# Eight tables that set the order of the engine calls in a four-layer diffusion step, replaced by others

## The chip, the cores and the metric

The kernel runs on one core of one Trainium2 chip. The metric is the device time of one execution in microseconds (us). Before the change it is 3068.2 us, the median of three runs (3067.97 to 3069.68). Five engines work side by side, each through its own queue of instructions, in the order in which they were put there: TensorE (PE in the rows) multiplies matrices, VectorE (DVE), ScalarE (ACT) and GpSimd (POOL) work elementwise, SyncE (SP) issues most of the transfers. An instruction that waits for another engine holds up all that stands behind it in its own queue.

## The reference

One inference step over 640 tokens of 1024 features (128 context tokens, 512 latent tokens) in fp32, four layers with the mixers A, B, C, A, and an MLP after each:

```python
for i in range(DEPTH):                       # 4 layers; kind = i % 3: A, B, C, A
    sh, sc, gt, sh2, sc2, gt2 = split(silu(cond) @ w_ada[i] + b_ada[i], 6)   # for c_ctx and for c
    h = rmsnorm(x, norm_g[i, 0]) * (1 + sc) + sh
    # A: sliding-window GQA with a sink logit; B: latent attention (low-rank q and kv);
    # C: GQA with q and k normalised per head; all with rotary positions, 16 heads
    x = x + gt * (mixer(h) @ w_o)
    h2 = rmsnorm(x, norm_g[i, 1]) * (1 + sc2) + sh2
    x = x + gt2 * (square(relu(h2 @ w_mlp_in[i])) @ w_mlp_out[i])
y = rmsnorm(x, g_final)
```

The outputs are y for both groups of tokens and the new keys, values and latents of the context tokens.

## The kernel before

x lies in SBUF with the features on the partitions, 4 tiles of 2 x 320 tokens per half. Each matrix product goes in 128x128 weight tiles against 320 tokens (a half of the 640), and each fp32 product is three matmuls of reduced-precision parts: high by high, high by low, low by high. `Stream` carries the weights: SP loads 128x1024 of them into one of two buffers `wraw`, ACT rounds them to the high part (`wa<-wraw`, called "hi" below), DVE subtracts to get the low part (`wa<-wraw,wa`, "lo"), and PE runs 24 matmuls for one output tile and half ("a unit", 8 feature tiles times 3). A `wraw` buffer is free for the next load when its lo is done. Results stand in eight PSUM tiles (`ps`, `psl`) until DVE or ACT has read them.

The adaLN rows need 512 KB tiles of `w_ada` (`adaw`). In layer 0's start PE multiplies them (16 tiles, then 24 tiles `adan` during the projections that follow). From layer 0's output projection on, DVE does this beside the rest: per tile two reductions `junk<-adaw,cb`, one for each condition; POOL issues those loads.

A layer is split into phases, named in the code: "start" and "qkv" (the norm and the projections; layer 0 also "qkv2", mixer B "dq"), "attn", "oproj" (output projection, the next norm, the first MLP products), and the rest of the MLP, which belongs to no phase. `Kern.ordered` keeps all engine calls of a phase as a list, where consecutive calls of PE into the same PSUM tile form one item, and `Calls.replay` issues them in the order of a table of item numbers:

```python
def replay(self, order):
    kept, self.kept = self.kept, None
    for i in order or range(len(kept)):
        for c in kept[i][1]:
            self.make(*c)
...
order = ORDER.get(n) or n[2:] == "attn" and range(len(self.nc.kept))
```

The table holds for PE, DVE, ACT and POOL, and in "0 start" and "0 qkv" for SP too. For "1 attn" there is no table before: its 1344 items go in the order in which the planner of the attention wrote them (`PLAN`, `PairB`). All calls pass through one line, `Calls.make`, so every row of the profile has the line L276, and instructions are told apart by the tiles they write and read. Waits between engines follow from the data: a reorder changes no arithmetic and no tile, only who stands ahead of whom.

Of the kernel before, what the change touches and what calls it, by code (L numbers as in the profile page):

```python
# [41 lines left out]
ORDER = {  # L42
    "0 attn": """
# [20 lines left out]
    "0 oproj": """  # L64
# [9 lines left out]
    """,  # L74
    "0 qkv2": """
# [4 lines left out]
    """,  # L80
    "0 qkv": """
# [5 lines left out]
    """,  # L87
    "0 start": """
# [4 lines left out]
    """,  # L93
    "1 dq": """
# [6 lines left out]
    """,  # L101
    "1 oproj": """
# [9 lines left out]
    """,  # L112
    "2 attn": """
# [90 lines left out]
}  # L204
ORDER = {n: [int(i) for i in o.split()] for n, o in ORDER.items()}

# [1554 lines left out]
```

## Time and profile before

| | |
|---|---|
| median of three runs | 3068.2 us |
| the profiled execution | 3069.06 us, of which the span of the page is 3067.3 us |
| mean granted clock of TensorE | 0.991 of full speed |
| PE, DVE, ACT, POOL busy | 97%, 69%, 44%, 18% of the span |

The share is over the whole span. The phases run one after another, and only in those where PE has holes can an order gain or lose. A row of the timeline reads: start, duration, engine, line, operation and tiles, count, and in brackets the idle time before it and what ended that.

### The profile page before, as it was taken

The numbers are of one execution on the slowest core, as the hardware profiler recorded it, in microseconds if no ns is written. First come the engines' busy times: TensorE is split into PE (matmuls) and PEld (weight loads), VectorE is DVE, ScalarE is ACT, GpSimd is POOL, SyncE is SP. The second block draws the span as 40 slices with busy tenths as digits, with TensorE's granted clock in tenths as the row PEclk, the third lists the DMA queues.
The fourth block names the chain that finished last, engine by engine and source line by source line (L and its number), as shares of the span: only waits on it lengthen the run. The fifth ranks groups of instructions, "written<-read, shape, count | busy, mean of one in ns | idle before, by whom it ended". The sixth has DMA issues, their size and how long they took to land. (4 is left out here: it accounts for less than half of the span.)

```text
span 3067.3 us, 52256 instructions
## 1 busy us (share of the span) xinstructions
PE 2962.0 (97%) x20250; PEld 2884.7 (94%) x20250; DVE 2122.7 (69%) x4605; ACT 1339.0 (44%) x2836; POOL 548.0 (18%) x713
## 2 busy tenths in 40 slices
PE   6999999999999999999998999999999999999998
PEld 4888999999999989999997889999999899999998
DVE  5696767666788887767469988776747896533434
ACT  3384522323487753322347883332233593322331
POOL 1162000000044341000003660000000370000000
PEclk9999999999999999999999999999999999999999
DMA  8303344442121134444211013444431102222221
GB/s 300 130 1 124 103 145 152 149 149 96 40 60 47 37 125 163 147 152 148 84 55 45 10 43 118 146 150 152 144 93 49 46 1 83 90 72 74 76 76 49
DMA packets 88602, 300.72 MB, mean 98 GB/s; under 512 B 10977, under 2 KB 15281, under 8 KB 87969
## 3 DMA queue, kind: packets, MB, share of 16 engines
q1 hardware_dynamic: 64112, 210.22, 20.6%
q0 software_dynamic: 24240, 87.16, 8.7%
q8 instruction: 159, 2.61, 0.3%
q14 instruction: 91, 0.74, 0.1%
HBM read 288.53 MB, written 3.56 MB: 95 GB/s over the span
## 5 line engine op out<-in xcount | busy, mean ns | idle before, releaser
L276 PE MATMUL ps<-ar,wa 128*128 128x320 f32 x6736 | 1139.2, 311 | 16.4 <-DVE wa L276 8.7
L276 PE MATMUL psl<-ar,wa 128*128 128x320 f32 x6408 | 1084.3, 310 | 1.9 <-DVE ar L276 1.6
L276 PEld LDWEIGHTS ps<-ar,wa 128*128 128x128 f32 x6736 | 1030.0, 189 | 20.9 <-DVE wa L276 9.5
L276 PEld LDWEIGHTS psl<-ar,wa 128*128 128x128 f32 x6408 | 979.4, 188 | 3.4 <-DVE ar L276 2.3
L276 ACT ACTIVATE wa<-wraw 128x1024 fp32r<-128x1024 f32 (+3 forms) x350 | 360.0, 1030 | 965.2 <-PE psl L276 440.2
L276 DVE TENSOR_TENSOR wa<-wraw,wa 128x1024 fp32r<-128x1024 f32 (+3 forms) x346 | 416.7, 1204 | 291.8 <-ACT wa L276 290.8
L276 DVE CUSTOM_DVE_ANT_0 junk<-adaw,cb 128x1024 bf16<-128x1024 f32 x304 | 373.4, 1228 | 9.4 <-DMA adaw<-ada 8.9
L276 PE MATMUL psl<-ex,wa 128*128 128x320 f32 x1320 | 322.9, 314 | 5.1 <-DVE wa L276 2.0
L276 PE MATMUL ps<-ex,wa 128*128 128x320 f32 x1304 | 318.1, 313 | 5.5 <-DVE wa L276 3.3
L276 POOL TENSOR_TENSOR p<-p,st 128x640 f32<-128x640 f32 (+2 forms) x256 | 277.0, 1104 | 180.0 <-DVE st L276 144.7
L276 POOL DMA_DIRECT2D adaw<-ada x152 | 80.5, 530 | 1051.4 <-DVE mod L276 983.9
L276 PE MATMUL psl<-wa,ar 128*128 128x320 f32 (+3 forms) x1024 | 236.2, 335 | 17.0 <-DVE st L276 7.5
L276 PEld LDWEIGHTS psl<-ex,wa 128*128 128x128 f32 x1320 | 229.1, 189 | 9.4 <-DVE wa L276 2.3
L276 DVE TENSOR_TENSOR ar<-ps,ar 128x512 fp32r<-128x512 f32 (+3 forms) x416 | 223.2, 560 | 19.8 <-ACT ar L276 16.3
L276 PEld LDWEIGHTS ps<-ex,wa 128*128 128x128 f32 x1304 | 225.5, 189 | 9.8 <-DVE wa L276 4.2
L276 ACT ACTIVATE ar<-ps 128x512 fp32r<-128x512 f32 (+5 forms) x452 | 208.5, 489 | 56.1 <-PE ps L276 50.7
L276 DVE SCALAR_TENSOR_TENSOR x<-ps,mod,x 128x320 f32<-128x320 f32 (+2 forms) x264 | 107.2, 436 | 180.8 <-PE ps L276 180.6
L276 DVE SCALAR_TENSOR_TENSOR x<-psl,mod,x 128x320 f32<-128x320 f32 (+2 forms) x240 | 98.7, 436 | 192.3 <-PE psl L276 192.2
L276 ACT ACTIVATE p<-p,st 128x640 f32<-128x640 f32 (+2 forms) x256 | 190.6, 748 | 18.7 <-DVE st L276 8.6
L276 PEld LDWEIGHTS psl<-wa,ar 128*128 128x128 f32 x1024 | 166.0, 193 | 30.7 <-DVE st L276 14.9
L276 PE MATMUL ps<-cst,p 128*128 128x128 f32 x1088 | 155.2, 274 | 5.6 <-DVE wa L276 2.6
L276 DVE TENSOR_TENSOR usq<-relu 128x320 f32<-128x320 f32 x256 | 124.5, 487 | 44.5 <-ACT relu L276 42.6
(205 smaller groups left out, 2817.6 us busy)
## 6 DMA issues: line engine op xcount, KB each, us to landing
adaw<-ada POOLq DMA_DIRECT2D x152, 512.0 KB, 4.3
wraw<-win SPq DMA_DIRECT2D x128, 512.0 KB, 3.3
wraw<-wout SPq DMA_DIRECT2D x128, 512.0 KB, 3.3
wraw<-qkv SPq DMA_DIRECT2D x36, 512.0 KB, 3.6
wa<-adan SPq DMA_DIRECT2D x24, 512.0 KB, 5.1
wraw<-wo SPq DMA_DIRECT2D x24, 512.0 KB, 3.7
adaw<-ada SPq DMA_DIRECT2D x16, 512.0 KB, 8.4
ar<-wa SPq DMA_DIRECT2D x64, 80.0 KB, 2.1
```

What stands on the lines that cost most here:

```text
L276: return m(*a, **k)
```

## The change

The code stays; the dictionary `ORDER` changes. Eight of its tables hold other numbers: "0 start", "0 qkv", "0 qkv2", "0 oproj", "1 oproj", "2 qkv", "3 qkv", and "1 attn", which had none. The tables of the other phases ("0 attn", "1 dq", "2 attn", "2 oproj", "3 attn", "3 oproj") only stand elsewhere in the dictionary. The same instructions are issued, each as often as before.

```diff
 ORDER = {
...
+    "1 attn": """
...
-    "0 oproj": """
...
+    "0 oproj": """
...
```

Three places as the engines' queues have them. First SP at the very start of the program: `adaw` are the eight buffers for tiles of `w_ada` (the last number tells the buffer, 152 to 159), `x` the input in four pieces, `wraw` the first projection weights. Before:

```order
1 L276 DMA cst<-cst 128x384
2 L276 DMA adaw_3_155<-ada 128x1024
3 L276 DMA x<-x 128x4x320
...
5 L276 DMA wraw_0_61<-qkv 128x1024
...
7 L276 DMA adaw_1_153<-ada 128x1024
8 L276 DMA adaw_2_154<-ada 128x1024
9 L276 DMA x<-x 128x4x320 x3
10 L276 DMA wraw_1_62<-qkv 128x1024
11 L276 DMA adaw_0_152<-ada 128x1024
12 L276 DMA adaw_5_157<-ada 128x1024
13 L276 DMA adaw_4_156<-ada 128x1024
```

After:

```order
1 L316 DMA cst<-cst 128x384
2 L316 DMA adaw_0_152<-ada 128x1024
...
4 L316 DMA adaw_1_153<-ada 128x1024
5 L316 DMA adaw_2_154<-ada 128x1024
6 L316 DMA adaw_3_155<-ada 128x1024
7 L316 DMA adaw_4_156<-ada 128x1024
8 L316 DMA x<-x 128x4x320 x2
9 L316 DMA adaw_5_157<-ada 128x1024
...
13 L316 DMA adaw_0_152<-ada 128x1024
14 L316 DMA wraw_0_61<-qkv 128x1024
15 L316 DMA adaw_1_153<-ada 128x1024
```

The tile that PE takes first, adaw_0, moved from behind all four pieces of x and two weights to the front; two pieces of x moved far behind.

Second, DVE at the head of layer 0's output projection ("0 oproj"). `wa_1006` and `wa_111` are the lows of two weight pieces, the rows with `adaw` the reductions. Before:

```order
517 L276 TENSOR_TENSOR ar_87<-ps_74,ar_86 128x512
518 L276 TENSOR_TENSOR ar_87<-ps_72,ar_86 64x128 x2
519 L276 ISA junk,mod_0_169<-adaw_0_2674,cb 128x1024
...
533 L276 ISA junk,mod_0_169<-adaw_3_2677,cb 128x1024
534 L276 ISA mod_0_169 128x1
535 L276 TENSOR_TENSOR wa_1006<-wraw_1_62,wa_1005 128x1024
536 L276 SCALAR_TENSOR_TENSOR x<-psl_2_80,mod_0_166,x 128x192
537 L276 TENSOR_TENSOR wa_111<-wraw_0_61,wa_110 128x1024
```

After:

```order
519 L316 TENSOR_TENSOR wa_111<-wraw_0_61,wa_110 128x1024
520 L316 TENSOR_TENSOR ar_87<-ps_74,ar_86 128x512
521 L316 TENSOR_TENSOR ar_87<-ps_72,ar_86 64x128 x2
522 L316 ISA junk,mod_0_169<-adaw_0_2674,cb 128x1024
...
536 L316 ISA junk,mod_0_169<-adaw_3_2677,cb 128x1024
537 L316 ISA mod_0_169 128x1
538 L316 SCALAR_TENSOR_TENSOR x<-psl_3_81,mod_0_166,x 128x320
539 L316 SCALAR_TENSOR_TENSOR x<-psl_2_80,mod_0_166,x 128x192
540 L316 SCALAR_TENSOR_TENSOR x<-psl_1_79,mod_0_166,x 128x320
541 L316 TENSOR_TENSOR wa_1006<-wraw_1_62,wa_1005 128x1024
```

The low wa_111 went ahead of the eight reductions, wa_1006 stayed behind them with three reads of PSUM now ahead of it. On PE the two units that use wa_111 now stand ahead of the unit that uses wa_1006.

Third, DVE at the end of layer 3's projections ("3 qkv"), around the last two lows, wa_1006 and wa_111; the other rows are rotary products and sums (`rps`, `rpq`, `ar`). Before:

```order
3707 L276 SCALAR_TENSOR_TENSOR ar_97<-rpq_0_21710,ar_97 64x320
3708 L276 TENSOR_TENSOR rpq_1_21711<-rpq_1_21711,rps_1_21709 128x192
3709 L276 STREAM_SHUFFLE rps_0_21708<-ps_71 128x320
3710 L276 TENSOR_TENSOR rpq_0_21710<-ps_71,tab_0_21700 128x320
3711 L276 SCALAR_TENSOR_TENSOR ar_97<-rpq_1_21711,ar_97 64x320
3712 L276 SCALAR_TENSOR_TENSOR ar_96<-rpq_1_21711,ar_96 64x320
3713 L276 TENSOR_TENSOR rpq_0_21710<-rpq_0_21710,rps_0_21708 128x320
3714 L276 STREAM_SHUFFLE rps_1_21709<-ps_72 128x192
3715 L276 TENSOR_TENSOR rpq_1_21711<-ps_72,tab_0_21700 128x192
3716 L276 TENSOR_TENSOR wa_111<-wraw_1_62,wa_110 128x1024
```

After:

```order
3710 L316 TENSOR_TENSOR wa_1006<-wraw_0_61,wa_1005 128x1024
3711 L316 TENSOR_TENSOR wa_115<-ck_1_21705,wa_1004 128x128
3712 L316 TENSOR_TENSOR rpq_0_21710<-rpq_0_21710,rps_0_21708 128x320
3713 L316 TENSOR_TENSOR wa_117<-ck_0_21704,wa_113 128x128
3714 L316 STREAM_SHUFFLE rps_0_21708<-ps_71 128x320
3715 L316 TENSOR_TENSOR wa_111<-wraw_1_62,wa_110 128x1024
3716 L316 TENSOR_TENSOR rpq_1_21711<-rpq_1_21711,rps_1_21709 128x192
3717 L316 TENSOR_TENSOR wa_116<-ck_0_21704,wa_112 128x128
3718 L316 STREAM_SHUFFLE rps_1_21709<-ps_72 128x192
```

Between the two lows stood thirteen rotary instructions; now four short ones stand there. On ACT the hi of wa_111 (`wa_110`) went ahead of the roundings of `ar_96` and `ar_97` in the same way.

## Rows read from the trace of the kernel before

**Rows 1.** The page's first part: busy time, share, instructions.

```profile
PE 2962.0 (97%) x20250; PEld 2884.7 (94%) x20250; DVE 2122.7 (69%) x4605; ACT 1339.0 (44%) x2836; POOL 548.0 (18%) x713
```

**Rows 2.** Stretches: before PE, start, qkv, qkv2, 0 oproj, MLP, 1 attn, 1 oproj, 2 qkv, 3 qkv.

```profile
core 0: us, PE busy (x) PEld busy (x) DVE busy (x) ACT busy (x) POOL busy (x), PEclk, DMA share, GB/s
0.00:20.49 20.49, 0.00 (x0) 0.03 (x1) 3.78 (x13) 6.58 (x13) 1.97 (x7) 1.00 0.93 329
20.49:55.60 35.11, 30.70 (x252) 22.08 (x253) 24.93 (x66) 14.37 (x33) 4.80 (x9) 0.95 0.85 310
55.60:104.46 48.86, 43.52 (x416) 34.08 (x415) 31.47 (x76) 18.64 (x42) 7.34 (x9) 1.00 0.73 253
104.46:153.80 49.34, 45.60 (x291) 45.07 (x290) 37.87 (x92) 21.37 (x51) 11.97 (x15) 0.93 0.18 60
252.85:386.75 133.90, 126.13 (x845) 124.80 (x844) 96.31 (x198) 52.27 (x105) 6.36 (x12) 0.96 0.40 135
386.75:782.60 395.85, 395.85 (x2701) 395.43 (x2700) 266.44 (x486) 109.99 (x176) 25.87 (x49) 1.00 0.40 132
841.12:1090.85 249.73, 238.58 (x1761) 233.36 (x1761) 211.92 (x512) 194.96 (x458) 113.26 (x105) 1.00 0.17 46
1090.85:1187.75 96.90, 93.23 (x625) 91.02 (x626) 85.88 (x169) 48.03 (x96) 30.33 (x29) 1.00 0.48 166
1580.23:1699.30 119.07, 103.38 (x654) 94.65 (x653) 106.84 (x243) 79.24 (x186) 38.45 (x44) 0.99 0.15 48
2342.55:2441.81 99.26, 91.35 (x618) 89.35 (x617) 81.04 (x207) 45.75 (x108) 20.96 (x30) 0.95 0.19 57
```

**Rows 3.** PE's waits from 0 to 56 us: for whom, total, times, longest.

```profile
PE ps L276 <- DMA adaw<-ada: 23.6, 2, 20.5
```

**Rows 4.** DMA from 2 to 40 us: GB/s in 40 slices, then the sum.

```profile
GB/s 317 372 255 238 293 361 385 408 404 391 365 365 364 365 375 403 414 405 405 405 414 293 341 310 259 276 323 375 410 414 423 423 418 410 397 405 410 410 414 410
DMA packets 5609, 14.08 MB, mean 371 GB/s; under 512 B 653, under 2 KB 2849, under 8 KB 5608
```

**Rows 5.** PE's waits in "0 qkv" (55.6 to 104.5 us).

```profile
PE ps L276 <- DMA wa<-adan: 2.4, 3, 1.1
```

**Rows 6.** PE's timeline at the end of "0 qkv2".

```profile
137.97 1.93 PE L276 MATMUL ps<-ar,wa 128*128 128x320 f32 x12
...
144.21 0.90 PE L276 MATMUL ps<-ex,wa 128*128 128x320 f32 x2 [3.34 <-DVE wa L276]
...
147.04 3.40 PE L276 MATMUL ps<-ar,wa 128*128 128x320 f32 x12
```

**Rows 7.** DVE's timeline at the same place: the low.

```profile
142.94 1.22 DVE L276 TENSOR_TENSOR wa<-wraw,wa 128x1024 fp32r<-128x1024 f32 x1
```

**Rows 8.** PE's timeline in "0 oproj", 262 to 292 us.

```profile
270.46 3.98 PE L276 MATMUL ps<-ar,wa 128*128 128x320 f32 x26
281.09 11.20 PE L276 MATMUL ps<-ar,wa 128*128 128x320 f32 x57 [6.66 <-DVE wa L276]
```

**Rows 9.** DVE's timeline there, first reduction and low; a group of the page's part 5.

```profile
269.80 1.23 DVE L276 CUSTOM_DVE_ANT_0 junk<-adaw,cb 128x1024 bf16<-128x1024 f32 x1 [5.18 <-DMA adaw<-ada]
...
279.82 1.22 DVE L276 TENSOR_TENSOR wa<-wraw,wa 128x1024 fp32r<-128x1024 f32 x1
...
L276 DVE SCALAR_TENSOR_TENSOR x<-psl,mod,x 128x320 f32<-128x320 f32 (+2 forms) x240 | 98.7, 436 | 192.3 <-PE psl L276 192.2
```

**Rows 10.** DVE's waits in "1 attn": for whom, total, times, longest.

```profile
DVE wa L276 <- ACT wa L276: 12.8, 17, 2.0
DVE ar L276 <- ACT ar L276: 6.9, 16, 1.1
```

**Rows 11.** The late part of "2 qkv" as a stretch, columns as in Rows 2.

```profile
1650.00:1699.30 49.30, 40.66 (x269) 37.27 (x268) 45.74 (x99) 32.92 (x75) 17.43 (x20) 0.98 0.16 56
```

**Rows 12.** PE's waits in "3 qkv" (2342 to 2442 us).

```profile
PE psl L276 <- ACT wa L276: 3.3, 1, 3.3
PE psl L276 <- DVE wa L276: 2.8, 2, 1.5
```

More of the change, by code (lines that the diff above doesn't have):

```diff
@@ L42 @@
 ORDER = {
+    "2 attn": """
[21 rows of a table added]
+    """,
+    "1 attn": """
[38 rows of a table added]
+    """,
+    "1 oproj": """
[9 rows of a table added]
+    """,
+    "1 dq": """
[6 rows of a table added]
+    """,
+    "3 qkv": """
[9 rows of a table added]
+    """,
+    "2 qkv": """
[13 rows of a table added]
+    """,
+    "0 oproj": """
[9 rows of a table added]
+    """,
+    "0 qkv2": """
[4 rows of a table added]
+    """,
+    "0 qkv": """
[5 rows of a table added]
+    """,
+    "0 start": """
[4 rows of a table added]
+    """,
     "0 attn": """
@@ L63 @@
     """,
-    "0 oproj": """
[9 rows of a table removed]
-    """,
-    "0 qkv2": """
[4 rows of a table removed]
-    """,
-    "0 qkv": """
[5 rows of a table removed]
-    """,
-    "0 start": """
[4 rows of a table removed]
-    """,
-    "1 dq": """
[6 rows of a table removed]
-    """,
-    "1 oproj": """
[9 rows of a table removed]
-    """,
-    "2 attn": """
[21 rows of a table removed]
-    """,
     "2 oproj": """
@@ L145 @@
         323 300 339 335 301 337 322 336 324 314 316 325 315 346 330 317 331 338 340 341 332 333
-    """,
-    "2 qkv": """
[13 rows of a table removed]
     """,
@@ L191 @@
         277 289 288 282 299 300 294 283 284 285 290 301 305 295 297 302 317 306 312 303 313 315 314 296 298 316 307 308 309 318 319 310 311
-    """,
-    "3 qkv": """
[9 rows of a table removed]
     """,
```

198 rows, old and new, of the table ORDER are left out of this document.

## The prediction

> **What bounds the kernel now.** I read the page's busy shares first: PE works 97% of the span, the next engine 69% [rows 1]. So the time is PE's work plus PE's holes, and since the change adds and removes no instruction, it can only act on holes and on the clock that follows them. Then I cut the span into the phases whose tables change and took, in each, the length less PE's busy time [rows 2]: 20.49 us before the first matmul, then 4.41 in the start, 5.34 in "0 qkv", 3.74 in "0 qkv2", 7.77 in "0 oproj", 11.15 in "1 attn", 3.67 in "1 oproj", 15.69 in "2 qkv" (with the wait at its end, by which "2 attn" starts), 7.91 in "3 qkv". The MLP's stretch has none. Behind the first matmul that makes 59.7 us. The clock column adds to it: where it says 0.93, 0.96 and 0.95, TensorE ran part of the stretch at 1.2 instead of 2.4 GHz, (1 - 0.93) / 0.5 x 49.34 = 6.9 us of "0 qkv2", by the same sum 10.7 us of "0 oproj" and 9.9 us of "3 qkv". Last I read, in each phase, for whom PE waited; these rows are named with the terms. The sum below is made against the profiled execution, 3069.06 us; the median is 0.86 lower.
>
> **The change, phase by phase.** Negative is time saved.
>
> *Start.* PE's first matmul waits 20.5 us for a tile `adaw`, and again 3.1 later [rows 3]. Nothing is idle there but PE: the transfers run all the while, 14.08 MB from 2 to 40 us at 371 GB/s on the mean, and 397 to 423 GB/s in the last slices [rows 4]. The changed SP order puts adaw_0 to adaw_4 first and half of x behind the second group. PE then works on each tile as it lands and gives the buffers back early, so the dip in the middle of the GB/s row (259 to 341), which I read as SP waiting for a free buffer, should close. At 410 GB/s the same 14.08 MB take 34.3 us instead of 38: the last tile lands 3.7 us earlier, and PE's products of the normed x, which no longer queue behind the tiles' matmuls, close up some 1.3 us of the 4.41 of holes. I take -5. Bounds: 0 (transfers no denser, the same bytes) and -8 (3.7 + 4.41).
> The Trainium skill ("DMA: Bandwidth & Descriptors", "Where 436 GB/s comes from") says that transfers from HBM to SBUF are bound by about 358 GB/s per core, below the ceiling of the on-chip fabric. By that the stretch, already at 371, would gain nothing and the sum would be 5 less. The rows with 397 to 423 GB/s speak against it, so it gets no case of its own.
>
> *"0 qkv".* 2.4 of the 5.34 are waits for tiles `adan` [rows 5], which the new table spreads out earlier. Four buffers go round, so a tile's load still waits for PE's use of the one before. I take -3, between -5.3 and +1.
>
> *"0 qkv2".* PE waits 3.34 for a low that DVE starts at 142.94 [rows 6, 7]. In the new order five short DVE instructions that stood ahead of that low stand behind it, and about two others now come ahead of it; at 0.44 us for a pass over 320 columns [rows 9] that is 3 x 0.44 = 1.3 us, and the wait of the first of them for ACT falls away. I put the low 1.9 us earlier. At half clock the 12 matmuls at 147.04 took 3.40 instead of 1.93 at full clock, and the 12 before them 147.04 - 144.21 = 2.83, so the dip cost about 2.4. Whether a hole of 1.5 to 2 still brings it, the rows don't decide. I take -2.5: the hole's part and a quarter of the dip. Bounds 0 and -6.1 (3.7 + 2.4).
>
> *"0 oproj".* The one large hole. DVE does eight reductions from 269.80 on, 10.0 us with what follows, and only then the low that PE waits for: 6.66 us [rows 8, 9]. PE had stopped at 274.44, with two units left over that need only wa_111, whose hi and load are long there. The change puts wa_111's low ahead of the reductions, where DVE sat idle 5.18 us, and it puts these two units ahead on PE: 48 matmuls x 0.153 us (3.98 / 26 [rows 8]) = 7.3 us more work, up to 281.8. Behind the reductions three reads of PSUM of 0.44 us and the low of 1.22 end at 279.82 + 1.3 + 1.22 = 282.3; with some 0.3 us from DVE to PE that leaves about 1 us of wait, so -5.6. The dip behind the hole goes too: 57 matmuls in 11.20 us against 57 x 0.153 = 8.7, so -2.5. Also, wa_111's buffer `wraw` is free 16 us earlier, so the next weights come earlier. -8.1, of which I take -7.5 for other small waits. Bounds -2 (the hole reappears at the next low) and -10.2 (6.66 + 1.1 for the phase's other holes + 2.5).
>
> *"1 attn".* 11.15 us of holes in many places; DVE waits 17 times for ACT's rounding (12.8 us) and 16 times for ACT's rows `ar` (6.9) [rows 10]. In 249.73 us PE works 238.58, DVE 211.92 and ACT 194.96 [rows 2]: these three hand each other short pieces, and a table replaces the planner's order. The moves are mostly of a few places; a unit of the values goes ahead of the score units in several spots, which fills holes of about 1 us. No row shows the new order's waits. Bounds -11 (all holes) and +8 (12.8 + 6.9 again by four tenths); I take -3, near the middle of the bounds.
>
> *"1 oproj".* A one-row sum behind an elementwise add went behind a unit on PE, and the order of the norm's rows puts the one that PE waits for earlier. Of 3.67 I take -1.5, bounds -3.7 and +2.
>
> *"2 qkv".* Here DVE is nearly the bound: 106.84 of 119.07 us, and 45.74 of 49.30 in the late part [rows 2, 11]. PE's 15.69 us of holes can go only as far as DVE's 12.2 idle us go; in the late part that is 3.6. The two weight conversions stand earlier and the last unit of values moved to the front, so its evacuation is no longer the last thing. I take -4, bounds -12 and +2.
>
> *"3 qkv".* PE waits 3.3 for a hi and 2.8 for two lows [rows 12], all in one unit. Between the lows stood thirteen rotary instructions; four short ones stand there now, so at 0.44 us [rows 9] DVE has the second low some 4 us sooner, and ACT the hi about as much. One us of wait is left of 6.1: -5. The half clock took 9.9 us of the stretch, 4.7 of them idle: 5.2 / 2 = 2.6 lost; most goes with the hole, -2. The rotary work pushed back runs beside the units that follow; DVE has 99.26 - 81.04 = 18.2 us of idle time in this phase to take it. -7, bounds -2 and -10.5.
>
> Sum: -5 - 3 - 2.5 - 7.5 - 3 - 1.5 - 4 - 7 = -33.5, so 3035.6 for the profiled execution and about **3035** us as a median.
>
> **Rivals.** *A, given back (25%).* What PE gains it waits for at the next gate, since DVE's queue is unchanged in length: "2 attn" already starts with a wait for DVE, and so does "0 attn". Speaks for it: DVE's share in "2 qkv" and "1 oproj" (85.88 of 96.90). Against: DVE has 11 us of idle time or more in the other projections [rows 2]. Then about half of "0 oproj", "3 qkv" and the start stays (10) and 6 of the rest: 3068 - 16 = 3052.
> *B, "1 attn" turns slower (6%).* If each of DVE's 17 and 16 waits for ACT took its longest value, 2.0 and 1.1 us, they would be 51.6 instead of 19.7: +31.9 in place of -3. It decides as soon as it eats the 30 us of the other phases. With the others at half (-15): 3068 + 32 - 15 = 3085. For it: DVE works 85% and ACT 78% of that stretch. Against: the moves are short.
> *C, the holes only move (7%).* Each unit put forward meets the next operand that is late; then only a few us of the start remain: 3065.
> The main case has 62%, its own range is 3020 to 3048.
>
> **How the numbers follow.** The sums of the bounds are far apart (-66 and +9), but they don't all fall together; the main case and A fill 3014 to 3058 but for their edges, with B and C outside: that is the range. Three runs of this kernel lie within 0.06%, and I call 0.2% (6 us) the least that can be told. Faster, below 3062: the main case and A, 0.88 with a little of C. Within 0.2%: 0.07. Slower: 0.05.
>
> **What would show it.** In the changed profile: the first matmul at about 5 us instead of 20.49, and the start's end near 50; no wait over 2 us near the reductions of "0 oproj" and no low clock there; one hole of about 1 us in place of three at the end of "3 qkv"; PE's holes in "1 attn" below 11 us. It is wrong if the wait at the start of "2 attn" or "3 attn" grows by what the projections gained, or if "1 attn" takes more than 250 us from its first to its last matmul.

## The result, and the profile after

The changed kernel takes 3095.7 us (median of 4 runs, 3091.5 to 3098.5), the kernel before 3068.1 beside it: ratio 1.0089, 95% interval 1.0072 to 1.0107. It is 27.6 us slower; I had forecast 33 us faster. Its profiled execution took 3091.5 us. The engines' shares, against [rows 1]:

```profile
PE 2978.4 (96%) x20250; PEld 2892.6 (94%) x20250; DVE 2122.8 (69%) x4605; ACT 1339.6 (43%) x2836; POOL 547.6 (18%) x713
```

DVE, ACT and POOL work as long as before. PE's 16.4 us more go to the same 20250 matmuls; the mean granted clock is 0.989 instead of 0.991, and how much of the 16.4 us that makes was not worked out. The stretches, against [rows 2]: before PE, start, "0 qkv", "0 qkv2", "0 oproj", "1 dq" with "1 attn", "1 oproj", "2 qkv", "3 qkv". ("1 dq" and "1 attn" are taken together, since the new order puts the first unit of "1 attn" between the last ones of "1 dq".)

```profile
0.00:6.26 6.26, 0.00 (x1) 0.01 (x1) 0.97 (x6) 1.50 (x2) 1.98 (x7) 1.00 0.68 226
6.26:48.45 42.19, 33.63 (x216) 20.84 (x217) 23.99 (x59) 17.04 (x36) 4.67 (x8) 0.92 0.97 361
48.45:96.23 47.78, 45.05 (x418) 36.23 (x416) 33.19 (x82) 21.66 (x48) 7.77 (x10) 1.00 0.79 284
96.23:146.77 50.54, 47.01 (x327) 45.62 (x323) 39.14 (x98) 21.51 (x51) 12.23 (x15) 1.00 0.18 54
247.10:769.60 522.50, 519.43 (x3544) 517.55 (x3543) 362.57 (x684) 162.53 (x280) 32.41 (x61) 1.00 0.41 135
769.60:1095.42 325.82, 298.11 (x2110) 286.26 (x2109) 248.72 (x627) 219.29 (x525) 116.07 (x108) 0.98 0.15 43
1095.42:1190.00 94.58, 87.38 (x575) 85.25 (x574) 77.63 (x157) 43.28 (x88) 26.51 (x29) 0.96 0.46 156
1596.71:1716.64 119.93, 105.55 (x652) 98.30 (x653) 101.29 (x230) 76.09 (x182) 37.88 (x45) 0.95 0.12 40
2366.44:2465.10 98.66, 93.23 (x619) 91.65 (x619) 76.84 (x195) 42.19 (x103) 22.39 (x33) 0.95 0.15 50
```

Not every stretch holds the matmuls of its counterpart: the start has 216 instead of 252, which stand in the two phases behind it, and "1 oproj" 575 instead of 625; with the next 50 it takes 102.2 us against 96.9.

The same two stretches of the kernel before that [rows 2] cut otherwise, "0 oproj" with its MLP and "1 dq" with "1 attn":

```profile
252.85:782.60 529.75, 521.98 (x3543) 520.23 (x3542) 362.75 (x684) 162.27 (x280) 32.23 (x61) 0.99 0.40 133
782.60:1090.85 308.25, 291.55 (x2111) 285.44 (x2109) 251.50 (x631) 220.74 (x528) 115.89 (x109) 0.99 0.17 46
```

So by the end of layer 0's MLP the changed kernel is 13.0 us ahead (769.60 against 782.60), and by the end of "1 attn" 4.6 us behind (1095.42 against 1090.85): 17.6 us are lost there. In layer 0, "0 oproj" did what I had said: the wait of 6.66 us [rows 8] is now two, and the clock stays at 2.4 GHz (1.00). PE's timeline there:

```profile
268.59 7.50 PE L316 MATMUL ps<-ar,wa 128*128 128x320 f32 x50
277.71 3.49 PE L316 MATMUL ps<-ar,wa 128*128 128x320 f32 x22 [1.63 <-DVE wa L316]
281.04 7.50 PE L316 MATMUL psl<-ar,wa 128*128 128x320 f32 x50
289.80 7.01 PE L316 MATMUL psl<-ar,wa 128*128 128x320 f32 x46 [1.26 <-DVE wa L316]
```

Two losses stand at the heads of phases, where I had not looked, and one near the end of "3 qkv". PE's timeline at the start of "2 qkv", at the start of "3 qkv" and near its end:

```profile
1596.71 1.44 PE L316 MATMUL psl<-ones,acc 128*128 128x1 f32 x6 [5.97 <-DVE acc L316]
...
2366.44 1.44 PE L316 MATMUL psl<-ones,acc 128*128 128x1 f32 x6 [6.09 <-DVE acc L316]
...
2439.25 0.56 PE L316 MATMUL ps<-ex,wa 128*128 128x320 f32 x2 [3.08 <-DVE wa L316]
```

Both new tables put the norm's row sum of the second half, item 0, first on PE. It needs DVE's last addition of squares, which is 6 us off; before, two units of the first half ("2 qkv") or three ("3 qkv") stood ahead and hid it. In "2 qkv" before, without a wait:

```profile
1587.27 0.72 PE L276 MATMUL psl<-ones,acc 128*128 128x1 f32 x6
```

The waits lie just ahead of the stretches above, which begin with these matmuls. Behind each wait PE goes on at half clock; the six matmuls take 1.44 us.

Third, "1 attn". Its waits after, in PE's, DVE's and ACT's views of 816.78 to 1095.42 us (for whom, total, times, longest), against [rows 10]:

```profile
PE ps L316 <- DVE ar L316: 7.3, 11, 1.5
PE ps L316 <- DVE wa L316: 5.1, 6, 1.8
```

```profile
DVE ar L316 <- ACT ar L316: 22.5, 31, 2.8
DVE wa L316 <- ACT wa L316: 11.0, 14, 1.3
```

```profile
ACT wa L316 <- DVE wa L316: 9.8, 11, 1.7
ACT ar L316 <- DVE ar L316: 9.8, 6, 2.9
```

The last two rows have no counterpart before: there ACT never waits for an `ar` or `wa` of DVE. ACT makes the high parts, DVE the low ones from them; what ACT should want of DVE's lows is the question of the experiments.

### The profile page after: what moved, and what is told of

It is laid out like the page before. It is cut to its first block, busy times and chain, and to the rows that moved or that the text cites. A ratio compares the mean times of both kernels' runs of the same rounds, so it can differ in the third digit from the quotient of the medians.

```text
span 3089.8 us, 52200 instructions
## 1 busy us (share of the span) xinstructions
PE 2978.4 (96%) x20250; PEld 2892.6 (94%) x20250; DVE 2122.8 (69%) x4605; ACT 1339.6 (43%) x2836; POOL 547.6 (18%) x713
## 4 chain that ended last, share of the span: by engine, by line
PE 58%; DVE 7%; ACT 4%; issue 1%; DMA 1%; POOL 0%; SPq 0%; DVEq 0%; ACTq 0%; POOLq 0%
PE ps L316 31%; PE psl L316 28%; DVE ar L316 2%; DVE wa L316 2%; ACT ar L316 1%; ACT wa L316 1%; ACT p L316 1%; DVE p L316 1%; DVE rpq L316 0%; DVE junk L316 0%; DVE hsq L316 0%; DMA wraw<-wout 0%; DVE rps L316 0%; DVE x L316 0%; DMA wraw<-wo 0%
## 5 line engine op out<-in xcount | busy, mean ns | idle before, releaser
L316 PEld LDWEIGHTS ps<-ar,wa 128*128 128x128 f32 x6736 | 1031.4, 189 | 21.3 <-DVE wa L316 8.1
```

The source lines that it names most:

```text
L316: return m(*a, **k)
```

## The experiments

Each is the kernel before with some tables exchanged, unless said otherwise; times are medians, and the kernel before was timed beside each group (3066.3 to 3067.8 us).

**Which part costs what.** *Layer 0 alone:*

```diff
 ORDER = {
-    "0 start", "0 qkv", "0 qkv2", "0 oproj": the numbers of before
+    "0 start", "0 qkv", "0 qkv2", "0 oproj": the numbers of the change
```

> The kernel before with the changed tables of layer 0 alone (0 start, 0 qkv, 0 qkv2, 0 oproj). Theory (each phase's effect adds up; in the changed kernel's trace PE stood 13.0 us earlier than before at the end of layer 0's output projection, and kept that through the MLP): 3055 us, -13. Rival (the gain is given back later, where the unchanged phases wait for DVE): 3064 to 3068.

3057.0 us, ratio 0.9972 (0.9961 to 0.9982): 9.3 us faster, of the 18 forecast for these four tables.

*"1 attn" alone:*

```diff
+    "1 attn": the numbers of the change
```

> The kernel before with the new table of 1 attn and nothing else. Theory M (the table itself is slow, whatever stands before and after it): the phase takes 273 to 280 us with about 25 us of holes of PE, 1 dq and 1 attn together grow by 15 to 23 us, and the time is 3083 to 3092 us. Rival E (the phase is slow in the changed kernel because the earlier phases hand it over in another state): below 258 us for the phase, 3068 to 3076 us.

3089.1 us, ratio 1.0077 (1.0060 to 1.0094): 21.3 us slower. The stretches ("1 dq" with "1 attn", then "1 attn"):

```profile
779.83:1108.73 328.90, 298.68 (x2111) 286.44 (x2109) 250.70 (x631) 220.62 (x528) 117.75 (x111) 0.98 0.15 45
827.29:1108.73 281.44, 253.04 (x1791) 241.19 (x1789) 218.82 (x535) 197.37 (x466) 117.75 (x111) 0.98 0.15 42
```

The table is slow by itself, whatever stands ahead of it.

*"1 oproj" alone:*

```diff
-    "1 oproj": the numbers of before
+    "1 oproj": the numbers of the change
```

> The kernel before with the new table of 1 oproj alone. Theory (its own order makes the waits for a row sum, for a low and for dg): the phase's holes go from 3.6 to about 7 us and a stretch at half clock follows, 3071 to 3075 us. Rival (it is slow only behind the new 1 attn): holes at or below 3.6 us, 3065 to 3068 us, as I had predicted of it (-1.5).

3069.6 us, ratio 1.001 (1.000 to 1.002): 1.8 us slower, between the two theories and hardly clear of noise. The profile shows two of the three waits that the theory named, for `dg` and for a row sum (`acc`); the wait for a low is 0.3 us as before. PE's, in this phase (before, all its waits were 1.3 us or shorter, 4.6 together):

```profile
PE psl L276 <- DVE dg L276: 2.6, 1, 2.6
PE psl L276 <- DVE acc L276: 1.5, 1, 1.5
PE ps L276 <- POOL ar L276: 1.4, 1, 1.4
```

*The heads of "2 qkv" and "3 qkv",* in the changed kernel: item 0 goes back behind two units on PE. All else keeps its place in its queue (but for one rounding of ACT, by one place); the list between the engines is woven anew.

```diff
 "2 qkv", PE's items:
-0 63 61 71 8 10 ...
+63 61 0 71 8 10 ...
 "3 qkv", PE's items:
-0 61 74 8 10 12 ...
+61 74 0 8 10 12 ...
```

> The changed kernel with one PE item moved in each of two tables: the matmul that sums the squares (psl<-ones,acc) goes behind the two units that the new tables put behind it, at the head of 2 qkv and of 3 qkv. Theory (the two waits of 6.0 and 6.1 us for acc, and the half clock behind them, are the cost of the heads: PE fell back by 10.6 and 8.7 us there): about 3096 - 17 = 3079 us. Rival (the hole only moves to the rows of the norm, which come later now): 3090 or more.

3086.0 us, ratio 1.0064 (1.0049 to 1.0079): 9.7 us less than the changed kernel (7.7 by the two ratios), between theory and rival: I expected 17. In PE's timeline the head of "2 qkv" runs through, now at full clock (the row sum's six matmuls take 0.72 us). The head of "3 qkv" is mended only in part: with two units ahead of item 0 instead of three, PE waits there for the norm's rows, 3.10 us for `dg` and then 1.00 for `nt` (before: 0.75 for `dg`), as the rival had it. Near the end of "3 qkv" the wait for the low is still there:

```profile
1587.73 9.40 PE L316 MATMUL psl<-ar,wa 128*128 128x320 f32 x63
...
1604.01 0.72 PE L316 MATMUL psl<-ones,acc 128*128 128x1 f32 x6
...
2371.56 1.22 PE L316 MATMUL psl<-dg,cst 128*128 128x128 f32 x4 [3.10 <-DVE dg L316]
...
2436.61 0.90 PE L316 MATMUL ps<-ex,wa 128*128 128x320 f32 x2 [3.44 <-DVE wa L316]
```

*"2 qkv" and "3 qkv" with these mended heads, in the kernel before:*

```diff
-    "2 qkv", "3 qkv": the numbers of before
+    "2 qkv", "3 qkv": the numbers of the change, item 0 behind two units
```

> The kernel before with the tables of 2 qkv and 3 qkv, their heads mended as in e2. Theory (what I forecast for the late parts holds; PE made up 3.4 us in each phase behind the head in the changed kernel's trace): 3068 - 7 = 3061 us. Rival (the late parts bring nothing by themselves, what PE gained there was only the room that the hole at the head had made): 3068 or more.

3070.6 us, ratio 1.0018 (1.0009 to 1.0028): 4.3 us slower, as the rival had it. Its reason does not hold for "3 qkv": up to the same matmul the head, with the waits just named, takes 25.87 us instead of 19.71, and the rest of the phase 3.5 us less. The rest before, then in this kernel:

```profile
2362.26:2441.81 79.55, 72.40 (x488) 70.66 (x487) 64.29 (x163) 38.74 (x92) 18.04 (x27) 0.94 0.14 44
```

```profile
2369.02:2445.07 76.05, 71.62 (x488) 70.77 (x487) 62.07 (x154) 36.28 (x87) 17.81 (x28) 0.96 0.15 48
```

"2 qkv" takes 120.3 us instead of 119.1. The waits that I had aimed at shrink there (at its end for `VS` from 3.5 to 1.8 us, for weights from 3.2 to 1.1), but those for the squares `hsq` grow from 7.0 to 10.5. So of the late parts, on which I had put -11, "3 qkv" brings 3.5 us and "2 qkv" nothing, and the head of "3 qkv" still loses 6.2.

These five add up: -9.3 + 21.3 + 1.8 + 9.7 + 4.3 = 27.8, where the whole change is 27.6. That they meet so closely is luck: each term is good to 3 to 5 us, and by the ratios the five make 1.0102 where the whole is 1.0089.

**Why "1 attn" is slow.** *PE's new order alone,* the other engines in the planner's:

```diff
 "1 attn":
-no table
+PE's items as in the change, DVE's, ACT's, POOL's and SP's as in the planner's list, woven into one list
```

> The kernel before with the new table's order in 1 attn for PE alone; DVE, ACT and POOL keep the planner's order. In the changed kernel PE lost 22 us in this phase. Theory P (PE's new order asks for operands before DVE and ACT make them): 3068 + 15 to 22 us. Theory D (the new order of DVE and ACT is what costs): 3068 to 3072.

3134.3 us, ratio 1.0217 (1.0200 to 1.0234): 68 us slower, missed by both theories. I read it then as "PE's order fits only with DVE's". That was too quick: weaving a new list had changed more than PE's order, as the last two runs show, so what PE's order does by itself stays open.

*The overtaken readers put back.* In most of PE's holes, as I read the queues, the DVE or ACT instruction that it waits for had been overtaken, in its own queue, by others.

```diff
 "1 attn" of the change:
-DVE: ... 143 136 ... 159 154 ... 1161 1160 ... 1177 1170 ...; ACT: ... 321 314 ... 833 809 808 823 812 815 804 ...
+DVE: ... 136 143 ... 154 159 ... 1160 1161 ... 1170 1177 ...; ACT: ... 314 321 ... 804 833 809 808 823 812 815 ...
```

> The same with 17 instructions of that table put back: those of DVE and ACT that free or make what PE waits for, each ahead of the ones that overtook it on its engine; PE's, POOL's and SP's orders stay the new ones. Theory R (the overtaken readers make the holes): 25 us of holes fall to 11 to 16, the half clock at the start of the phase goes, and the time is 10 to 16 us below that of the run with the whole new table, 3070 to 3078 us. Rival S (DVE and ACT are late throughout, and a mended reader only moves the hole to the next one): holes above 20 us, less than 5 us below that run.

3100.0 us, ratio 1.0110 (1.0095 to 1.0125): 11 us slower than the whole new table, and the holes of "1 attn" grow from 28.4 to 290.24 - 256.73 = 33.5 us:

```profile
830.96:1121.20 290.24, 256.73 (x1790) 246.25 (x1788) 220.23 (x535) 197.60 (x466) 117.69 (x110) 0.96 0.14 41
```

Neither theory had that: R had the time fall, S had it stay. But this list was woven anew as well: around item 310 it reads 310 316 327 268 326 337 312, where the change has 310 324 316 348 312 338 314. By the next two runs such weaving alone moves the time by 10 and by 28 us, so what the overtaking costs stays open.

*Only the order between engines.* That left ACT's waits for DVE. I looked in the compiled programs for what each of them waits on: in 18 places of the new "1 attn" an ACT instruction waits for a DVE instruction with which it shares no result, only a PSUM tile that both read. Before there is 1 such place. (The two kernels below have 18, in part others, and 27: the count alone does not set the cost.) Who of two readers waits depends on which is called first in the list; the planner calls all of ACT's roundings of a tile and then DVE's lows, while the table often puts a low between two roundings. So two kernels in which no instruction of PE, DVE, ACT or POOL changes its place in its queue (of SP's issues a few neighbours change places):

```diff
 "1 attn" of the change, each engine's items in the same order, woven anew:
-... 313 315 335 310 324 316 348 312 338 314 ...
+... 313 311 310 309 312 320 324 315 314 331 316 ...
```

> The kernel before with the new table of 1 attn, in which PE's, DVE's, ACT's and POOL's own orders are the new ones and only the order of the calls between engines differs: each call stands where it would start by the durations of the trace if two engines that read the same tile of PSUM had not to wait for each other. Theory L (of two readers of one tile the one that is called later waits for the other, and the table calls DVE's low ahead of ACT's next rounding too often): ACT's waits for DVE fall from 20 us to below 12, PE's holes from 25 to 14 to 18 us, and the time is 7 to 14 us below that of the run with the whole new table, 3075 to 3082 us. Rival Q (the engines' own orders make the loss): within 4 us of that run, 3085 to 3093 us.

```diff
 "1 attn" of the planner, each engine's items in the same order:
-... 310 311 312 313 314 315 316 ...
+... 310 311 348 349 350 377 318 516 312 319 313 315 320 316 314 ...
```

> The kernel before, with PE, DVE, ACT and POOL in 1 attn each in the planner's own order, instruction for instruction; only between engines DVE's calls are put about 1 us earlier, so that DVE's low is called ahead of ACT's next rounding of the same tile of PSUM in 27 places instead of 1 (SP's issues differ by a few neighbours that change places). Theory L: ACT waits for DVE in 1 attn for over 15 us instead of 8, PE's holes go from 11 to over 22 us, and the time is 14 to 28 us above before, 3082 to 3096 us. Rival Q: no engine's order has changed, so within 3 us of before, 3065 to 3071 us.

The first: 3079.2 us, ratio 1.0043 (1.0028 to 1.0058), 9.9 us less than the whole new table (10.4 by the ratios). The second: 3094.1 us, ratio 1.0090 (1.0072 to 1.0107), 27.7 us slower than before. Q expected nothing of either. The stretch of "1 attn" and ACT's waits in it, first kernel:

```profile
827.87:1098.81 270.94, 249.95 (x1791) 238.93 (x1789) 219.79 (x535) 197.98 (x466) 117.45 (x110) 0.99 0.16 43
```

```profile
ACT wa L316 <- DVE wa L316: 4.9, 9, 0.8
...
ACT ar L316 <- DVE ar L316: 3.0, 2, 2.2
```

Second kernel:

```profile
837.28:1117.63 280.35, 252.30 (x1761) 240.13 (x1761) 210.42 (x512) 194.27 (x458) 113.25 (x105) 0.97 0.15 41
```

```profile
ACT wa L316 <- DVE wa L316: 17.8, 20, 1.2
ACT ar L316 <- DVE ar L316: 14.7, 21, 1.4
```

ACT's waits for DVE's `ar` and `wa`, and the time, stand in one order: 0 and 3068 before, 7.9 and 3079 in the first kernel, 19.6 and 3089 with the whole new table, 32.5 and 3094 in the second; PE's holes are 11.2, 21.0, 28.4 and 28.0 us. Where PE's, DVE's or ACT's queues differ too, that order does not hold: with the overtaken readers put back ACT's waits are 17.5 us and the time 3100, with PE's new order alone 23.2 and 3134. What is shown is each pair with the same queues. In the second kernel the stretch grows by 30.6 us: 16.9 are holes of PE, 13.7 the same 1761 matmuls taking longer at a granted clock of 0.97 instead of 1.00; and DVE's waits for ACT's `ar` and `wa` grow too, from 19.7 to 37.4 us. One place shows it instruction by instruction. ACT's and then DVE's timeline in the kernel before, at the tile that items 310 to 316 read:

```profile
900.50 1.48 ACT L276 ACTIVATE wa<-ps 64x384 fp32r<-64x384 f32 x3
902.00 0.83 ACT L276 ACTIVATE p<-p,st 128x640 f32<-128x640 f32 x1
```

```profile
902.01 1.12 DVE L276 TENSOR_TENSOR wa<-ps,wa 64x384 fp32r<-64x384 f32 x2 [0.59 <-ACT wa L276]
```

And in the second kernel ACT's, DVE's and PE's:

```profile
905.82 0.98 ACT L316 ACTIVATE wa<-ps 64x384 fp32r<-64x384 f32 x2
907.99 0.48 ACT L316 ACTIVATE wa<-ps 64x384 fp32r<-64x384 f32 x1 [1.19 <-DVE wa L316]
908.50 0.83 ACT L316 ACTIVATE p<-p,st 128x640 f32<-128x640 f32 x1
```

```profile
906.84 1.12 DVE L316 TENSOR_TENSOR wa<-ps,wa 64x384 fp32r<-64x384 f32 x2 [0.38 <-ACT wa L316]
```

```profile
908.53 0.66 PE L316 MATMUL ps<-cst,p 128*128 128x128 f32 x4 [1.10 <-ACT wa L316]
```

The queues are the same. Before, ACT's roundings of the tile follow one another, and DVE's two lows come behind them; then the tile is free. With DVE called first, ACT's last rounding starts 30 ns behind DVE's lows, 1.2 us late, and PE, which wants the tile for its next transposes, waits 1.10 us (before 0.40). The rounding takes nothing from the lows.
The Trainium skill ("PSUM — Partial Sum Buffer", "PSUM bank collisions raise a hardware error") says that a scheduler adds a dependency between any two instructions on different engines that touch the same bank and quadrant, "reads and writes alike". The trace agrees in this place: the wait is between two reads. Whether they could be left out was not tried.

**What wins.** The tables of "0 start", "0 qkv" and "0 oproj", and of "3 qkv" two moves: the hi and the low that [rows 12] wait for go ahead of the rotary pieces. Beside them, two matmuls go some 100 matmuls later on PE, and one hi of the values with its low goes ahead by a few places; what these do was not measured apart.

```diff
 "3 qkv", ACT's items:
-... 290 277 275 285 287 283 299 297 312 ...
+... 290 277 275 312 285 287 283 299 297 ...
 "3 qkv", DVE's items:
-... 291 276 278 286 282 288 296 293 295 300 298 306 302 304 313 320 ...
+... 291 313 276 278 286 282 288 296 293 295 300 298 306 302 304 320 ...
```

> The kernel before with the new tables of 0 start, 0 qkv and 0 oproj, without that of 0 qkv2, and in 3 qkv with two moves alone: ACT's hi and DVE's low of the second weight tile of the last unit with 320 columns go ahead of the rotary pieces between. Theory: layer 0 gives 9 to 11 us as with qkv2's table, and in 3 qkv the holes of 3.3 and 1.4 us at the unit that waited for that low close, 4 to 5 us with them; 3052 us (3049 to 3055). Rival G (given back: the rotary pieces pushed behind are what 3 attn waits for next): 3 attn's holes grow by what 3 qkv's shrink, 3056 to 3059 us.

3052.3 us, ratio 0.9952 (0.9937 to 0.9967): 15.5 us faster than before and 43 faster than the change. "3 qkv" with "3 attn", before and then in this kernel; 199.58 - 195.69 = 3.9 us:

```profile
2342.55:2542.13 199.58, 190.55 (x1278) 180.05 (x1276) 175.99 (x501) 135.89 (x363) 87.79 (x135) 0.97 0.10 32
```

```profile
2330.13:2525.82 195.69, 190.37 (x1278) 180.46 (x1276) 174.95 (x501) 135.56 (x363) 87.87 (x135) 0.98 0.10 32
```

## Why the prediction was wrong

*Start, mis-sized.* First matmul at 6.26 (said: about 5), the start's end at 48.45 (said: near 50), 7.2 us earlier. But 36 matmuls of the start now stand behind that mark. By equal count little is gained: PE has done 252 matmuls at 54.00 instead of 55.60 us, 1.6 of the 5 forecast. The transfers are denser, as I had read from the slices with 397 to 423 GB/s, and PE's matmuls on the last tile `adaw` begin 3.9 us earlier (35.73 against 39.66; 3.7 forecast). The transfers of 2 to 40 us, against [rows 4]:

```profile
DMA packets 5824, 14.89 MB, mean 392 GB/s; under 512 B 675, under 2 KB 2865, under 8 KB 5823
```

The Trainium skill's bound of about 358 GB/s ("DMA: Bandwidth & Descriptors", "Where 436 GB/s comes from"), as that section gives it, does not hold here, then: 392 on the mean. What failed is the rest of the term, that PE's holes would close up: they are 8.6 instead of 4.4 us, since PE now works at the transfers' pace, and the start has more of the half clock (0.95 to 0.92). PE's waits from 0 to 48.5 us:

```profile
PE ps L316 <- DMA adaw<-ada: 5.5, 7, 3.8
```

"0 qkv" and "0 qkv2" take 98.3 us together against 98.2, but with the 36 matmuls more (5.5 us at 0.153 us each [rows 8]). The half clock that [rows 6] show in "0 qkv2" is gone in this profile (0.93 to 1.00), not wholly in the one with layer 0's tables alone (0.97); its wait of 3.34 us is now three, of 0.70, 1.87 and 0.95.
Over the profiled executions with the old tables of layer 0 (eight) and with the new (four, one of them without that of "0 qkv2"), PE has done 252 matmuls at 55.9 and 55.1 us on the mean, "0 qkv2" ends at 153.2 and 149.7, and "0 oproj" begins at 253.1 and 250.6: -0.8, -3.5 and -2.6 of the -10.5 that I had forecast for the three. I had counted each phase's holes as if the one ahead did not hand them on; that is rival A, but in these phases themselves, since only 0.9 us are given back behind them.

*"0 oproj", right:* -7.5 forecast, 7.3 in the profile of the change, 8.7 in that of the best kernel (521.04 us). One allowance in this term, 0.3 us from DVE to PE, no row shows: in [rows 8, 9] PE starts 0.05 us behind the low.

*"1 attn", the step that failed.* I took -3, "near the middle of the bounds", because "the moves are mostly of a few places", and bounded it at +8. It is +21.3. I had read each engine's queue, and the sentence ahead of the prediction that waits follow from the data and that a reorder only changes who stands ahead of whom is half of it: the list orders readers on different engines too. The failure I had named as rival B, with 6%, and with a price not far off (+32 forecast, 21 measured), in part by luck, since I had it as DVE waiting for ACT: those waits grew from 19.7 [rows 10] to 33.5 us; the 19.6 us of ACT for DVE were not in it. Re-weaving the list takes back about half (9.9 of 21.3). What the rest is, the runs leave open: in that kernel DVE still waits more for ACT and PE's holes are 21.0 instead of 11.2 us.

*"2 qkv" and "3 qkv", a step left out.* I looked at the waits that the change takes away, at the late ends, and not at the first thing that each new table does on PE. Moving the row sum back gave 9.7 us, with part of the loss still standing in "3 qkv".

*The late ends, mis-sized.* For "3 qkv" I expected one hole of 1 us in place of three, and that came true for the unit that I had looked at (0.28 and 0.45 us). But the table also moves the low ahead of it, and the unit before waits 3.08 us: rival C, the hole moved. The late part of the whole table gave 3.5 us and the two moves of the best kernel 3.9, of the 7 forecast. In "2 qkv" nothing came of -4: PE waits for `hsq` what it no longer waits for the weights and `VS`, rival C again.

*"1 oproj":* -1.5 forecast, +1.8 measured, hardly clear of noise; the row sum and the norm's `dg` that I had thought hidden are waited for.

The signs that I had named told it rightly: "1 attn" above 250 us and with more holes than 11 (278.64 and 25.9).

## What to carry to other kernels

A list of calls for several engines holds more than each engine's order: for two engines that read the same PSUM tile it says who waits, so keep the readers of one engine together, the one whose result the other needs first, and compare waits in both directions. Read a new order at the first instruction of each phase, not only where the old one waited. Compare phases by the matmuls done, since a reorder also moves the marks between phases. A wait that has one row and one cause could be sized from the trace in "0 oproj" (7.3 and 8.7 us for 7.5 forecast), to half in "3 qkv" (3.5 and 3.9 for 7), and not in "0 qkv2", where it split into three. A phase that three engines share in pieces of 0.5 us could not be sized here from their idle time.

## What the runs showed of the hardware

With no queue of PE, DVE, ACT or POOL changed, the order of the calls between engines moved the time by 27.7 us. "1 dq" was left as it was, and yet the same matmuls took 58.5 us at a clock of 0.94 before and 56.4 at 0.97 in the kernel with DVE first:

```profile
782.60:841.12 58.52, 52.97 (x350) 52.08 (x348) 39.58 (x119) 25.79 (x71) 2.63 (x5) 0.94 0.17 50
```

```profile
780.91:837.28 56.37, 51.34 (x350) 50.66 (x348) 39.62 (x119) 25.90 (x71) 2.62 (x5) 0.97 0.16 52
```

Such stretches at half clock come and go from kernel to kernel. In the six profiles in which no queue of "1 dq" and "1 attn" changed, "1 dq" takes 55.1 to 58.5 us, and in the eight with the old tables of layer 0, "0 oproj" begins between 250.7 and 257.7 us. So a position in one profile is good to 3 to 7 us, and what is smaller needs timed runs.
